# The last stage of a two-layer decoder trunk: output chunks in tiles of their own, an earlier first store, and a root with a bias

## The chip, the cores and the metric

The kernel runs on one NeuronCore of a Trainium2 chip. Its engines work side by side, each through a queue of its own: TensorE (PE, matmuls; PEld are its weight loads), VectorE (DVE), ScalarE (ACT), GpSimd (POOL) and SyncE (SP, which here only issues transfers). [...] The metric is the device time of the whole kernel in microseconds, the median of several runs.

## The reference, cut to what matters

Two layers of token mixers, cross-attention and gated MLPs work on x, 512 tokens of 1024 channels in float32. The change concerns the end of the second layer: the residual add of the last MLP's down projection, and the final norm.

```
h = rms_norm(x, norm) @ w_up
g = causal_dwconv(h[..., :D_FF], dw_w, dw_b)
u = h[..., D_FF:]
x = x + (gelu(g) * u) @ w_down
...
y = x * rsqrt(mean(x * x, axis=-1) + 1e-6)      # per token, over 1024 channels
return y * final_norm                           # per channel
```

## The kernel before, in words

x is kept transposed: eight tiles `X[n]` of 128 channels (partitions) by 512 tokens, all in the one SBUF tile `xall`. Every weight and activation is split into a high and a low part, and each product is three matmuls (`mm3`, lines 185 to 187). Layers, attention and MLP come one after the other; the MLP's gated values are computed in six groups, and the last group's down projection is left to `finish` (line 1098), which is also the final norm. There the 512 tokens are treated in two ways.

*The first 384 tokens* (`TC`) stay transposed. The loop from line 1105 makes, for each of the eight chunks n, 12 matmuls, adds the result to `X[n][:, :TC]` (line 1115, VectorE), squares it (line 1117, ScalarE) and sums the squares over the chunks (line 1122).

*The last 128 tokens* are turned round, tokens on partitions: TensorE transposes their x (line 1113), and `xt`, a 128 by 1024 tile, takes them. The down projection for them comes in four pieces of 256 channels: `last(j)` (line 1128) makes 12 matmuls, and `added(j)` (line 1134) adds the piece to `xt` on VectorE, and squares it on ScalarE with a sum over the piece's channels into column j of the small tile `sm` (in the trace an ACTIVATE and a read of the accumulator). For pieces 0 and 1 GpSimd also multiplies by the channels' gains (line 1139). `count(j)` (line 1141) adds column j-1 to column j, so that column 3 ends as the sum over all channels.

From line 1156 on, the order of the work is written out by hand: within `manual_schedule` each engine, and SP's queue of transfers, executes its instructions in the order of the program text. In that order:

- Piece 0; then 12 small matmuls (line 1161) that sum the squares of the first 384 tokens over the channels, a root (line 1163), a reciprocal (line 1164), and `diagonals` (line 324) and `spread` (line 345), which bring 1/rms of every token to all 128 partitions: two matmuls (line 348) into `r`, a PSUM tile of 128 by 384.
[...]
- `normed(n)` (line 1144) finishes a chunk in its place in x. For n = 3, 5, 7 ScalarE multiplies by the gain (line 1147) and GpSimd by `rs` (line 1148). For the others VectorE does both in one instruction with `r` (line 1150).
- `store(n)` (line 1152) issues one transfer for chunks n and n+1 on SP's queue, 128 partitions by two rows of 1.5 KB. There are four; the first follows chunks 0 and 1.
- Among these stand `added(2)` and `added(3)` and the counts. After count(3) come the root (line 1188, ScalarE), the reciprocal (line 1189, VectorE), and the last multiplications: ScalarE for the first 512 channels (line 1190), VectorE for the rest with the gains (line 1192). One transfer for each half (lines 1191 and 1193) ends the kernel.

VectorE's order there: count(1), normed(0), normed(1), normed(2), added(2), normed(4), count(2), added(3), normed(6), count(3), reciprocal, last multiplication.

Of the kernel before, what the change touches and what calls it, by code (L numbers as in the profile page):

```python
# [12 lines left out]
AF = mybir.ActivationFunctionType  # L13
ALU = mybir.AluOpType

P = 128
T = 512

TC = 384
D = 1024  # L20
C = D // P
# [6 lines left out]
EPS = 1e-6  # L28
# [32 lines left out]
def trunk(ctx: ExitStack, tc: tile.TileContext, I: dict, out: list):  # L61
    nc = tc.nc
    V, A, G, PE = nc.vector, nc.scalar, nc.gpsimd, nc.tensor
# [14 lines left out]
    def nm(s):  # L78
        uid[0] += 1
        return f"{s}_{uid[0]}"  # L80
# [7 lines left out]
    def big_f():  # L88
        return big.tile([P, 2 * T], F32, tag="big", name=nm("big"))
# [4 lines left out]
    def tmp_f(n=T):  # L94
        return tmp.tile([P, n], F32, tag="tmp", name=nm("tmp"))
# [4 lines left out]
    def aux_ps():  # L100
        return aux.tile([P, T], F32, tag="aux", name=nm("aux"))
# [3 lines left out]
    def mm_ps():  # L105

        wide[1] += 1
        return aux_ps() if wide[0] and wide[1] % 7 in (2, 5) else main_ps()

    def stat_ps():  # L110
        return stat.tile([P, T], F32, tag="stat", name=nm("stat"))


    eps = cpool.tile([P, 1], F32, tag="eps", name="eps")
# [4 lines left out]
    xall = xpool.tile([P, C, T], F32, tag="x", name="x")  # L119
    X = [xall[:, c] for c in range(C)]  # L120

    def col(name, i=0):
        j = _COL[name] + i
        return par[:, j : j + 1]
# [21 lines left out]
    def load_w(src=None, eng=None, raw=None, parts=1, ahead=AHEAD, park=False):  # L146

        with tc.high_priority(ahead):
            if raw is None:
                raw = wp.tile([P, D], F32, tag="raw", name=nm("raw"), bufs=3)  # L150
                fetched[0] = nc.sync.dma_start(raw, src)
            if park:
                both = [split(raw[:, i : i + T], None, None, eng) for i in (0, T)]
                return [b[0] for b in both], [b[1] for b in both]
            hi = wp.tile([P, D], F32R, tag="whi", name=nm("whi"))
            lo = wp.tile([P, D], F32R, tag="wlo", name=nm("wlo"))
            n = D // parts
            for i in range(0, D, n):
                split(raw[:, i : i + n], hi[:, i : i + n], lo[:, i : i + n], eng)
        return hi, lo  # L160
# [22 lines left out]
    def mm3(ps, w, x, first, last):  # L183
        (wh, wl), (xh, xl) = w, x
        PE.matmul(ps, wh, xh, start=first, stop=False)  # L185
        PE.matmul(ps, wh, xl, start=False, stop=False)  # L186
        PE.matmul(ps, wl, xh, start=False, stop=last)  # L187
# [16 lines left out]
    def blk(w, i, n=P):  # L204
        hi, lo = (w.hi, w.lo) if isinstance(w, Piece) else w
        if isinstance(hi, list):
            hi, lo, i = hi[i // T], lo[i // T], i % T
        return hi[:, i : i + n], lo[:, i : i + n]
# [27 lines left out]
    class Scaled:  # L236
# [20 lines left out]
        def spread(self):  # L257
            self.r = spread(self.d, unit if self.halves else onesf)
# [65 lines left out]
    def diagonals(rt, n=4, halves=True):  # L324

        def diagonal(out, v, scale):
            V.scalar_tensor_tensor(
                out.rearrange("p (a b) -> p a b", a=n), ident.unsqueeze(1).broadcast_to([P, n, P]), scale,
                v.unsqueeze(2).broadcast_to([P, n, P]), op0=ALU.mult, op1=ALU.mult,
            )  # L330

        if not halves:
            d = [tmp_f(n * P)]
            diagonal(d[0], rt, float(D))
            return d
        hi = small.tile([P, n], F32R, tag="rhi", name=nm("rhi"), bufs=1)
        lo = small.tile([P, n], F32, tag="rlo", name=nm("rlo"), bufs=1)
        d = [act_r()[:, : n * P] for _ in range(2)]
        V.tensor_copy(hi, rt)
        diagonal(d[0], hi.bitcast(F32), 1.0)  # L340
        V.tensor_tensor(lo, rt, hi.bitcast(F32), op=ALU.subtract)
        diagonal(d[1], lo, 1.0)
        return d
# [25 lines left out]
    class Memory:  # L369


        r = rt = None
# [725 lines left out]
    def finish(y, w):  # L1098


        w = [w] + [load_w(I["wdown"][(2 * NG - 1) * (C // 2) + j]) for j in range(1, C // 2)]
        gains = big_f()
        nc.sync.dma_start(gains, I["final_norm"])
        ss, st, xt = None, stat_ps(), big_f()
        for n in range(C):
            x = X[n][:, :TC]
            ps = mm_ps()[:, :TC]
            for k in range(GC):
                mm3(ps, blk(w[n // 2], (k * 2 + n % 2) * P), blk(y[k], 0, TC), k == 0, k == GC - 1)
            if n % 4 == 1:  # L1110
                at, h = aux_ps(), n // 4
                for i in range(4):
                    PE.transpose(at[:, i * P : (i + 1) * P], X[4 * h + i][:, TC:], ident)
                A.activation(xt[:, h * T : (h + 1) * T], at, AF.Copy)
            V.tensor_tensor(x, x, ps, op=ALU.add)
            sq = tmp_f(TC)
            A.activation(sq, x, AF.Square)
            if n == 1:

                A.activation(small.tile([P, 1], F32, tag="warm", name="root", bufs=1), sq[:, :1], AF.Sqrt)  # L1120
            if 0 < n < C - 1:
                V.tensor_tensor(sq, sq, ss, op=ALU.add)
            if n < C - 1:
                ss = sq
        sm = small.tile([P, 5], F32, tag="smt", name="smt", bufs=1)
        H = T // 2

        def last(j):
            ps = mm_ps()[:, :H]
            for k in range(GC):  # L1130
                mm3(ps, blk(y[k], TC), blk(w[j], k * 2 * P, H), k == 0, k == GC - 1)
            return ps

        def added(j, ps):
            at = slice(j * H, (j + 1) * H)
            V.tensor_tensor(xt[:, at], xt[:, at], ps, op=ALU.add)
            A.activation(tmp_f(H), xt[:, at], AF.Square, accum_out=sm[:, j : j + 1])
            if j < 2:
                G.tensor_tensor(xt[:, at], xt[:, at], gains[:, at], op=ALU.mult)

        def count(j):
            V.tensor_tensor(sm[:, j : j + 1], sm[:, j - 1 : j], sm[:, j : j + 1], op=ALU.add)

        def normed(n):
            x, g = X[n][:, :TC], col("final_norm", n)
            if n in (3, 5, 7):
                A.activation(x, x, AF.Copy, scale=g)
                G.tensor_tensor(x, x, rs, op=ALU.mult)
            else:
                V.scalar_tensor_tensor(x, x, g, r, op0=ALU.mult, op1=ALU.mult)  # L1150

        def store(n):
            o = out[0][n : n + 2].rearrange("c p t -> p c t")
            nc.sync.dma_start(o, xall[:, n : n + 2, :TC])

        with tc.manual_schedule(engines=ORDERED | {mybir.EngineType.SP}):
            added(0, last(0))
            n_b = TC // P
            for j in range(n_b):
                for s, first in ((ss, True), (sq, False)):  # L1160
                    PE.matmul(st[:, j : j + 1], s[:, j * P : (j + 1) * P], onesf[:, :1], start=first, stop=not first)
            rt = small.tile([P, 4], F32, tag="rtok", name=nm("rtok"), bufs=2)
            A.activation(rt[:, :n_b], st[:, :n_b], AF.Sqrt, bias=eps)
            V.reciprocal(rt[:, :n_b], rt[:, :n_b])
            d = diagonals(rt[:, :n_b], n_b)
            ps = last(1)
            r = spread(d, ps=aux_ps()[:, :TC])
            added(1, ps)
            rs = tmp_f(TC)
            A.activation(rs, r, AF.Copy)  # L1170
            count(1)
            normed(0)
            normed(3)
            normed(1)
            store(0)
            normed(2)
            normed(5)
            store(2)
            added(2, last(2))
            normed(4)  # L1180
            store(4)
            normed(7)
            count(2)
            added(3, last(3))
            normed(6)
            store(6)
            count(3)
            A.activation(sm[:, 4:], sm[:, 3:4], AF.Sqrt, bias=eps, scale=1.0 / D)
            V.reciprocal(sm[:, 4:], sm[:, 4:])
            A.activation(xt[:, :T], xt[:, :T], AF.Copy, scale=sm[:, 4:])  # L1190
            A.dma_start(out[1][:, :T], xt[:, :T])
            V.scalar_tensor_tensor(xt[:, T:], xt[:, T:], sm[:, 4:], gains[:, T:], op0=ALU.mult, op1=ALU.mult)
            nc.sync.dma_start(out[1][:, T:], xt[:, T:])
# [459 lines left out]
    with tc.manual_schedule(engines=ORDERED | {mybir.EngineType.SP}):  # L1653
# [20 lines left out]
        ps = [[mm_ps(), mm_ps()] for _ in range(2)]  # L1674
# [164 lines left out]
```

## Time and profile before

| | us |
|---|---|
| median of 3 runs (1432.86 to 1433.24) | 1432.87 |
| the profiled execution | 1434.17 |
| its span, first to last instruction | 1432.3 |
| TensorE busy in it (matmuls) | 1419.6 |
| VectorE busy | 1176.7 |
| ScalarE busy | 798.2 |
| GpSimd busy | 304.4 |

The profile is of one execution. Its span counts from the first to the last instruction, and its own time holds what lies around that too, so a sum made in the profile is set against 1434.17 and then carried over to the median. Names as in the text: "x<-x,par,aux" means that an instruction writes tile x and reads x, par and aux; L1150 is line 1150; in timelines the first figure is the start and the second the length in microseconds, and consecutive instructions of one kind may be drawn together (x3).

### The profile page before, as it was taken

Reading aid. Unit: us, or ns where it says so; the run is one execution under the profiler, and the core shown is the slowest. Engines: PE = TensorE matmul, PEld = TensorE weight load, DVE = VectorE, ACT = ScalarE, POOL = GpSimd, SP = SyncE. Lnnn points to the kernel's source line nnn. Section 1 sums busy time; section 2 is a strip of 40 time slices with the busy share of each in tenths; the row PEclk is TensorE's granted clock in tenths of the full one; section 3 lists DMA queues with packets and bytes.
Section 4 is the critical chain, followed back from the end, with each engine's and each line's share of the span. In section 5 each row is a group of like instructions: output and inputs, shape, how many; then the busy total and the mean of one; then the engine's idle time right before and its main releaser. Section 6 shows DMA issues by size and latency. Waiting matters only on the chain.

```text
span 1432.3 us, 22644 instructions
## 1 busy us (share of the span) xinstructions
PE 1419.6 (99%) x8504; PEld 1257.3 (88%) x8504; DVE 1176.7 (82%) x1955; ACT 798.2 (56%) x1321; POOL 304.4 (21%) x317
## 2 busy tenths in 40 slices
PE   9999999999999999999999999999999999999997
PEld 7888888998899999999988777899889999999997
DVE  6987776778788888888888997978778888888885
ACT  7678754666544444544565547767655444444434
POOL 0001310200021221222008992010001222222201
PEclk9999999999999999999999999999999999999999
DMA  8523232542557777777432464345244876787741
GB/s 292 198 81 99 93 118 81 118 111 89 158 136 169 162 182 165 163 173 173 136 123 89 118 167 143 107 87 147 87 129 121 178 179 157 171 184 159 162 126 59
DMA packets 77517, 200.11 MB, mean 140 GB/s; under 512 B 8672, under 2 KB 9952, under 8 KB 77408
## 3 DMA queue, kind: packets, MB, share of 16 engines
q1 hardware_dynamic: 50624, 150.15, 33.6%
q0 software_dynamic: 26496, 48.25, 20.5%
q8 instruction: 67, 1.10, 0.3%
q14 instruction: 42, 0.34, 0.1%
q10 hardware_dynamic: 288, 0.27, 0.1%
HBM read 145.16 MB, written 2.10 MB: 103 GB/s over the span
## 4 chain that ended last, share of the span: by engine, by line
PE 91%; DVE 3%; POOL 2%; DMA 2%; ACT 1%; issue 1%; SPq 0%; POOLq 0%; ACTq 0%; DVEq 0%
PE mm L186 22%; PE mm L185 22%; PE mm L187 22%; PE aux L185 7%; PE aux L186 7%; PE aux L187 7%; PE mm L456 2%; DMA raw<-in_wv 1%; DVE wlo L166 1%; POOL actf L1443 1%; PE aux L529 0%; ACT whi L165 0%; POOL act L166 0%; POOL tmp L1264 0%; DMA raw<-in_win 0%
## 5 line engine op out<-in xcount | busy, mean ns | idle before, releaser
L186 PE MATMUL mm<-act,whi 128*128 128x512 f32 (+2 forms) x1093 | 385.1, 352 | 0.6 <-DVE act L180 0.5
L185 PE MATMUL mm<-act,whi 128*128 128x512 f32 (+2 forms) x1093 | 384.6, 353 | 0.1
L187 PE MATMUL mm<-act,wlo 128*128 128x512 f32 (+2 forms) x1093 | 384.6, 352 | 0.0
L186 PEld LDWEIGHTS mm<-act,whi 128*128 128x128 f32 x1093 | 206.6, 189 | 30.3 <-DVE act L166 1.0
L185 PEld LDWEIGHTS mm<-act,whi 128*128 128x128 f32 x1093 | 206.4, 189 | 30.0 <-ACT tmp L1442 0.8
L187 PEld LDWEIGHTS mm<-act,wlo 128*128 128x128 f32 x1093 | 206.6, 189 | 27.0
L793 ACT ACTIVATE bigr<-raw 128x512 fp32r<-128x512 f32 x160 | 100.7, 630 | 156.7 <-DMA raw<-wa 64.3
L187 PE MATMUL mm<-bigr,bigr 128*128 128x256 f32 x640 | 181.1, 283 | 0.0
L186 PE MATMUL mm<-bigr,bigr 128*128 128x256 f32 x640 | 181.1, 283 | 0.0
L185 PE MATMUL mm<-bigr,bigr 128*128 128x256 f32 x640 | 180.9, 283 | 0.0
L170 DVE TENSOR_TENSOR tmp<-mm,tmp 128x256 f32<-128x256 f32 x322 | 131.2, 420 | 34.7 <-PE mm L187 28.3
L185 PE MATMUL aux<-act,whi 128*128 128x512 f32 x399 | 156.3, 392 | 0.0
L186 PE MATMUL aux<-act,whi 128*128 128x512 f32 x399 | 156.2, 391 | 0.0
L187 PE MATMUL aux<-act,wlo 128*128 128x512 f32 x399 | 155.2, 389 | 0.0
L165 ACT ACTIVATE whi<-raw 128x1024 fp32r<-128x1024 f32 (+1 forms) x95 | 96.6, 1021 | 85.5 <-PE mm L186 44.5
L800 DVE TENSOR_TENSOR bigr<-raw,bigr 128x512 fp32r<-128x512 f32 x160 | 110.0, 688 | 32.4 <-ACT bigr L793 30.4
L186 PEld LDWEIGHTS mm<-bigr,bigr 128*128 128x128 f32 x640 | 122.7, 192 | 1.6
L185 PEld LDWEIGHTS mm<-bigr,bigr 128*128 128x128 f32 x640 | 122.7, 192 | 1.6
L187 PEld LDWEIGHTS mm<-bigr,bigr 128*128 128x128 f32 x640 | 122.7, 192 | 0.0
L803 POOL DMA_DIRECT2D raw<-raw x46 | 39.8, 866 | 350.8 <-DVE wlo L800 303.9
L166 DVE TENSOR_TENSOR wlo<-raw,whi 128x1024 fp32r<-128x1024 f32 (+1 forms) x75 | 90.7, 1212 | 19.7 <-ACT whi L165 19.5
L807 POOL DMA_DIRECT2D raw<-wa x46 | 39.7, 864 | 303.2 <-DVE bigr L800 253.6
(341 smaller groups left out, 3013.4 us busy)
## 6 DMA issues: line engine op xcount, KB each, us to landing
raw<-wa POOLq DMA_DIRECT2D x138, 256.0 KB, 4.4
big<-in_wdown SPq DMA_DIRECT2D x42, 512.0 KB, 6.7
wa<-in_wpair SPq DMA_DIRECT2D x80, 256.0 KB, 3.4
raw<-in_wpair SPq DMA_DIRECT2D x40, 512.0 KB, 5.7
raw<-in_pw SPq DMA_DIRECT2D x24, 512.0 KB, 3.5
raw<-raw POOLq DMA_DIRECT2D x46, 256.0 KB, 7.3
raw<-in_win SPq DMA_DIRECT2D x20, 512.0 KB, 3.4
raw<-in_wk SPq DMA_DIRECT2D x16, 512.0 KB, 3.7
```

Source lines behind the costliest of these rows:

```text
L165: A.activation(hi, src, AF.Copy)
L166: fetched[1] = (eng or V).tensor_tensor(lo, src, hi.bitcast(F32), op=ALU.subtract)
L170: V.tensor_tensor(out, a, b, op=ALU.add)
L185: PE.matmul(ps, wh, xh, start=first, stop=False)
L186: PE.matmul(ps, wh, xl, start=False, stop=False)
L187: PE.matmul(ps, wl, xh, start=False, stop=last)
L456: PE.matmul(p, m[j], x, start=k == 0 and j == 0 and x is hi, stop=k == C - 1 and x is lo)
L793: A.activation(self.w[name][0], self.block(name), AF.Copy)
L800: V.tensor_tensor(lo, self.block(name), hi.bitcast(F32), op=ALU.subtract)
L803: G.dma_start(self.r, self.z, accum_op=ALU.add)
L807: G.dma_start(self.r, self.a22, accum_op=ALU.add)
L1443: G.tensor_tensor(z[:, s:], z[:, s:], f[:, s:], op=ALU.add)
```

## The change

- The finished chunks no longer overwrite x. Four new tiles `done` of 128 by 768 take two chunks each, side by side. The output tensor `out` is laid out the same way, 4 by 128 by 768, so that a store moves one contiguous row of 3 KB on each partition; the host puts the rows back in order.
- The first pair is stored in two halves, chunk 0 as soon as it is there. There are five stores in place of four.
- `rs` is made ahead of piece 1's square, and VectorE's chunks read `rs` in SBUF where they read `r` in PSUM.
- ScalarE's three gain multiplications (`gained`) go ahead of that copy.
- GpSimd's product for piece 1 (`weighed(1)`) goes behind its last chunk.
- VectorE's order becomes: added(1), normed(0), normed(1), normed(2), count(1), normed(4), added(2), normed(6), count(2), a new small instruction, added(3), reciprocal, last multiplication.
- count(3) goes. The new instruction makes (sum of pieces 0 to 2) / 1024 + 1e-6, and the last root takes this as its bias and piece 3's sum, times 1/1024, as its input.

```diff
@@ -1135,26 +1135,32 @@
             at = slice(j * H, (j + 1) * H)
             V.tensor_tensor(xt[:, at], xt[:, at], ps, op=ALU.add)
             A.activation(tmp_f(H), xt[:, at], AF.Square, accum_out=sm[:, j : j + 1])
-            if j < 2:
-                G.tensor_tensor(xt[:, at], xt[:, at], gains[:, at], op=ALU.mult)
 
         def count(j):
             V.tensor_tensor(sm[:, j : j + 1], sm[:, j - 1 : j], sm[:, j : j + 1], op=ALU.add)
 
+        done = [big_f()[:, : 2 * TC] for _ in range(C // 2)]
+
+        def weighed(j):
+            at = slice(j * H, (j + 1) * H)
+            G.tensor_tensor(xt[:, at], xt[:, at], gains[:, at], op=ALU.mult)
+
+        def gained(n):
+            A.activation(X[n][:, :TC], X[n][:, :TC], AF.Copy, scale=col("final_norm", n))
+
         def normed(n):
-            x, g = X[n][:, :TC], col("final_norm", n)
+            x, o = X[n][:, :TC], done[n // 2][:, n % 2 * TC : (n % 2 + 1) * TC]
             if n in (3, 5, 7):
-                A.activation(x, x, AF.Copy, scale=g)
-                G.tensor_tensor(x, x, rs, op=ALU.mult)
+                G.tensor_tensor(o, x, rs, op=ALU.mult)
             else:
-                V.scalar_tensor_tensor(x, x, g, r, op0=ALU.mult, op1=ALU.mult)
-
-        def store(n):
-            o = out[0][n : n + 2].rearrange("c p t -> p c t")
-            nc.sync.dma_start(o, xall[:, n : n + 2, :TC])
+                V.scalar_tensor_tensor(o, x, col("final_norm", n), rs, op0=ALU.mult, op1=ALU.mult)
+
+        def store(n, at=slice(0, 2 * TC)):
+            nc.sync.dma_start(out[0][n // 2][:, at], done[n // 2][:, at])
 
         with tc.manual_schedule(engines=ORDERED | {mybir.EngineType.SP}):
             added(0, last(0))
+            weighed(0)
             n_b = TC // P
...
             d = diagonals(rt[:, :n_b], n_b)
             ps = last(1)
             r = spread(d, ps=aux_ps()[:, :TC])
-            added(1, ps)
+            for n in (3, 5, 7):
+                gained(n)
             rs = tmp_f(TC)
             A.activation(rs, r, AF.Copy)
-            count(1)
+            added(1, ps)
             normed(0)
+            store(0, slice(0, TC))
             normed(3)
             normed(1)
-            store(0)
+            store(0, slice(TC, 2 * TC))
             normed(2)
+            store(2)
+            count(1)
             normed(5)
-            store(2)
-            added(2, last(2))
             normed(4)
             store(4)
+            added(2, last(2))
             normed(7)
-            count(2)
-            added(3, last(3))
             normed(6)
             store(6)
-            count(3)
-            A.activation(sm[:, 4:], sm[:, 3:4], AF.Sqrt, bias=eps, scale=1.0 / D)
+            weighed(1)
+            count(2)
+            V.tensor_scalar(sm[:, 4:], sm[:, 2:3], 1.0 / D, EPS, op0=ALU.mult, op1=ALU.add)
+            added(3, last(3))
+            A.activation(sm[:, 4:], sm[:, 3:4], AF.Sqrt, bias=sm[:, 4:], scale=1.0 / D)
             V.reciprocal(sm[:, 4:], sm[:, 4:])
             A.activation(xt[:, :T], xt[:, :T], AF.Copy, scale=sm[:, 4:])
             A.dma_start(out[1][:, :T], xt[:, :T])
@@ -1829,10 +1839,11 @@
-    shapes = {"out": (C, P, TC), "last": (T - TC, D)}
+    shapes = {"out": (C // 2, P, 2 * TC), "last": (T - TC, D)}
...
-    return np.concatenate([r["out"].reshape(D, TC).T, r["last"].reshape(T - TC, D)], axis=0).reshape(1, T, D)
+    first = r["out"].reshape(C // 2, P, 2, TC).transpose(3, 0, 2, 1).reshape(TC, D)
+    return np.concatenate([first, r["last"].reshape(T - TC, D)], axis=0).reshape(1, T, D)
```

## The prediction

> **What bounds the kernel now.** I read the page's chain of work first, then the chain of the last 14 us in order of time, then the timelines of VectorE, GpSimd, ScalarE and the queues there.
>
> ```profile
> PE 91%; DVE 3%; POOL 2%; DMA 2%; ACT 1%; issue 1%; SPq 0%; POOLq 0%; ACTq 0%; DVEq 0%
> ```
>
> TensorE carries 91% of the chain. The change touches no matmul, so it can only move what stands after the last ones.
>
> ```profile
> 1424.71 0.28 PE L187 MATMUL mm<-whi,act 128*128 128x256 f32 x1
> ```
>
> The last matmul ends at 1424.99 of a span of 1432.3: 7.3 us of tail is the whole stake. A faster tail can't bring more than some of that, and 0.2% of 1432.87, about what a measurement of this kernel can tell from no change, is 2.87 us. The chain through the tail:
>
> ```profile
> 1422.98 1.67 DVE x L1150 x3
> 1424.64 0.34 DVE big L1136
> ...
> 1425.71 0.34 DVE big L1136
> 1426.06 0.02 issue
> 1426.08 0.52 ACT tmp L1137 x2
> 1426.60 0.02 issue
> 1426.62 0.50 DVE smt L1142
> 1427.13 0.02 issue
> 1427.15 0.30 ACT smt L1188
> 1427.45 0.02 issue
> 1427.48 0.17 DVE smt L1189
> ...
> 1427.74 0.72 ACT big L1190
> ```
>
> It is VectorE's queue that sets it: three normed chunks, the addition of piece 2, a normed chunk, a count, the addition of piece 3 (ends at 1426.05); then square, count, root, reciprocal and the weighing, which ends at 1428.46: 2.41 us after that addition. Then come the transfers.
>
> ```profile
> 1424.15 0.41 SPq L1154 DMA_DIRECT2D out<-x  x1
> 1428.49 0.35 ACTq L1191 DMA_DIRECT2D last<-big  x1
> ```
>
> ```profile
> out<-x SPq DMA_DIRECT2D x4, 384.0 KB, 2.9
> ```
>
> ```profile
> 1425.00:1425.25 0.25, 0.00 (x0) 0.00 (x0) 0.25 (x1) 0.24 (x1) 0.25 (x1) 1.00 0.64 227
> 1425.00:1430.75 5.75, 0.00 (x0) 0.00 (x0) 2.92 (x7) 2.55 (x7) 1.51 (x2) 0.83 1.01 363
> ```
>
> The first fence is the queues' timeline, the second a row of the DMA issues (count, size, us to landing), the third a view by windows, whose last two columns are the DMA engines' share and their GB/s. The first store is issued at 1424.15; the window from 1425.00 is 64% full, so bytes flow from about 1425.09, 0.94 us later; and from there to 1430.75 the engines are full at 363 GB/s. The four stores (4 x 384 KB, 1.57 MB) take 4.3 of those microseconds, to about 1429.4. The last transfer, issued at 1428.49, could start 0.94 us later, at 1429.4. So computation and transfers end in a tie: making only one of them earlier gives nothing.
>
> **The change, part by part.** *The factor.* The normed chunks now take `rs` (SBUF) in place of `r` (PSUM), and the copy that makes it goes ahead of piece 1's square.
>
> ```profile
> 1421.68 0.44 PE L348 MATMUL aux<-act,unit 128*128 128x384 f32 x1 [0.16 <-DVE act L327]
> 1422.47 0.47 ACT L1170 ACTIVATE tmp<-aux 128x384 f32<-128x384 f32 x1
> 1422.06 0.42 ACT L1137 ACTIVATE tmp<-big 128x256 f32<-128x256 f32 x1 [2.10 <-DVE big L1136]
> ```
>
> `r` is there at 1422.12, so the copy runs from 1422.16 to 1422.63 and normed(0) starts at 1422.67 instead of 1422.98: 0.31 us gained. The three `gained` copies run in ScalarE's 2.10 us of idle time ahead of L1137 and cost nothing; without that cover they would cost some 0.5 us each.
>
> *VectorE and GpSimd.* The price lies here. Before, a normed chunk on VectorE read x from SBUF and r from PSUM. Now both inputs lie in SBUF, and GpSimd's products read two SBUF inputs at the same time. What the trace shows when both engines do that is in the mixer of the first layer (timeline: start, length, instruction):
>
> ```profile
> 181.25 1.21 DVE L166 TENSOR_TENSOR wlo<-raw,whi 128x1024 fp32r<-128x1024 f32 x1
> 182.38 1.78 DVE L166 TENSOR_TENSOR act<-tmp,act 128x512 fp32r<-128x512 f32 x1
> 181.52 2.08 POOL L1249 TENSOR_TENSOR tmp<-tmp,big 128x512 f32<-128x512 f32 x1 [1.28 <-ACT tmp L1246]
> 183.57 1.74 POOL L1249 TENSOR_TENSOR tmp<-tmp,big 128x512 f32<-128x512 f32 x1
> ```
>
> And two groups of the same sizes from stretches where the two engines were not both reading two SBUF inputs (behind the bar: us in all, then mean ns):
>
> ```profile
> L180 DVE TENSOR_TENSOR act<-tmp,act 128x512 fp32r<-128x512 f32 x6 | 4.2, 693 | 3.2 <-ACT act L175 3.2
> L1443 POOL TENSOR_TENSOR actf<-actf,tmp 128x510 f32<-128x510 f32 x5 | 6.5, 1297 | 0.0
> ```
>
> GpSimd starts at 181.52 while VectorE's L166 runs to 182.46, and ends at 183.60, 1.14 after it; such a product takes 1.30 alone. VectorE's next one, in the queue at 182.38, ends at 184.16, 0.56 after GpSimd; alone it takes 0.69. GpSimd's next ends 1.15 after that. They take turns, each waiting for the whole other one, and the engine that has waited goes next. A turn costs GpSimd its time less 0.15, VectorE its time less 0.13. The end of this kernel shows both sides of the rule:
>
> ```profile
> 1424.04 0.61 DVE L1150 SCALAR_TENSOR_TENSOR x<-x,par,aux 128x384 f32<-128x384 f32 x1
> 1423.53 1.99 POOL L1148 TENSOR_TENSOR x<-x,tmp 128x384 f32<-128x384 f32 x2
> 1425.55 0.16 DVE L1142 TENSOR_TENSOR smt<-smt 128x1 f32<-128x1 f32 x1
> 1426.10 1.00 POOL L1148 TENSOR_TENSOR x<-x,tmp 128x384 f32<-128x384 f32 x1 [0.59 <-ACT x L1147]
> 1426.62 0.49 DVE L1142 TENSOR_TENSOR smt<-smt 128x1 f32<-128x1 f32 x1
> ```
>
> With r in PSUM, L1150 took 0.61 in the midst of GpSimd's product. The count, two SBUF inputs of one element, took 0.49 instead of 0.16 and ended at 1427.11, as GpSimd did.
>
> [...]
>
> The pieces, from the rows of this stage:
>
> ```profile
> L1148 POOL TENSOR_TENSOR x<-x,tmp 128x384 f32<-128x384 f32 x3 | 3.0, 1011 | 0.7 <-ACT x L1147 0.6
> L1139 POOL TENSOR_TENSOR big<-big,big 128x256 f32<-128x256 f32 x2 | 1.5, 737 | 41.3 <-ACT tmp L1137 41.3
> L857 DVE SCALAR_TENSOR_TENSOR tmp<-tmp,par,tmp 128x511 f32<-128x511 f32 x40 | 29.8, 745 | 0.0
> L267 DVE SCALAR_TENSOR_TENSOR actf<-x,par,aux 128x512 f32<-128x512 f32 x16 | 11.9, 746 | 0.6 <-PE aux L348 0.6
> ```
>
> The last two rows say that the place of the second input (SBUF, 745 ns; PSUM, 746) costs nothing by itself, so a normed chunk stays at 0.61, or 0.53 behind another (three in 1.67). A turn is then 0.86 for GpSimd's 384 columns, 0.59 for its 256, 0.48 for a normed chunk, 0.03 for a count. I let VectorE start first, as it began 0.04 us after the copy's end here (if GpSimd does, the same turns end 0.1 later): normed(0) to 1423.28, normed(3) on GpSimd to 1424.14, normed(1) to 1424.62, normed(5) to 1425.48, normed(2) to 1425.96, normed(7) to 1426.82, count(1) to 1426.85, weighed(1) to 1427.44, normed(4) to 1427.92. GpSimd is then done. Three terms more: added(2), which reads PSUM, 0.34, to 1428.26; normed(6), 0.53, to 1428.79; count(2), 0.05 later and 0.16 long, to 1429.00 (its square, begun at 1428.29 and 0.52 long, is done by then). The new small `tensor_scalar` isn't shown; between nothing and twice the reciprocal's 0.17 with its 0.03 of issue, I take that row once: 1429.20. added(3), 0.34, ends at 1429.54 instead of 1426.05: **3.49 us later**. What is queued behind the blocked normed(1), normed(2) and normed(4) on VectorE are the two additions, and for these the last square waits.
>
> *The root with a bias.* Square to root now stay on ScalarE: 0.02 + 0.52 + 0.02 + 0.30, reciprocal 0.02 + 0.17, weighing 0.09 + 0.72: 1.86 in place of 2.41. **0.55 us gained**, of which 0.33 was the count's stall. weighed(1), moved behind normed(7), is done 3 us ahead of its reader.
>
> *Stores.* The first is issued near 1423.3, 0.8 us earlier, and there is one more issue (0.41) on an idle queue. But the last pieces are weighed at 1428.46 + 3.49 - 0.55 = 1431.40, and the stores are out of the way: the last two are issued at 1428.0 (behind normed(4)) and 1428.8 (behind normed(6)), and their bytes are through at about 1430.9, while the last transfer's start is 1432.4. Rows of 3 KB in place of 1.5 KB change only these stores, not the last pieces' own layout: if faster, they gain nothing at the end; if they halved the rate, the last two stores would need 2.2 us each and hold the last transfers up by 0.9 us. I take nothing, by the 363 GB/s that the engines already move. The tail behind the last issue stays at 3.8 us.
>
> **Sum:** +3.49 - 0.55 = +2.94 us. The profiled execution took 1434.17 with a span of 1432.3, so it would become 1437.1; it was 1.30 above the median of 1432.87, which becomes **1435.8**.
>
> **The rivals.**
>
> 1. *Turns in another order.* If normed(4) slips in right behind the one-element count(1), ahead of weighed(1), it ends at 1427.38, added(2) at 1427.72, weighed(1) at 1427.97 and normed(6) at 1428.45: 0.34 less, **1435.5**. [...] Against it: in the rows above the engine that had waited went next.
>
> 2. *Nothing overlaps.* If a blocked instruction takes its full time after the other's end, eight turns lengthen by 0.13 to 0.15 each: some +1.1, **1436.9**. Against it are the 1.14 and 0.56 us above. [...]
>
> [...]
>
> 4. *Not slower: the engines don't block each other here.* [...] It decides as soon as a normed chunk beside GpSimd's product keeps 0.61 us. [...]
>
> **How the numbers follow.** Chances: the turns as worked out 0.50, rival 1 0.20, rival 2 0.08, rival 3 0.08, rival 4 0.07, something upstream that moves with the new tiles and makes it slower still 0.04, a gain that no row shows 0.03. The bound for slower lies at 1435.74. Of the forecast's 0.50, its small terms (0.1 to 0.3 us in the gaps between instructions and the unseen `tensor_scalar`) put about two thirds above it, 0.34; with 0.05 of rival 1, rival 2's 0.08 and the 0.04 that is **0.51 slower**. Within 0.2% lie 0.16 + 0.15 + 0.08 + 0.07 = **0.46**; **0.03** is left for faster. The range runs from rival 3 to rival 2, 1434.0 to 1437.0, and leaves out 0.14.
>
> **What would show it.** Right: GpSimd's three products at 1.3 to 1.4 us each instead of 1.0; normed(1), (2) and (4) on VectorE at 1.3 us or more; added(3) ending some 3.5 us later; DMA engines with gaps before the last stores; no count ahead of the last root. [...] A shift ahead of 1417 us would mean that the new tiles touch earlier work, which I haven't priced.

## The result and the profile after

The changed kernel takes 1435.97 us (median of 16 runs), the kernel before 1432.51 (median of 16 runs between them): a ratio of 1.0022, 95% interval [1.0014, 1.0029], or +3.2 us with an interval from +2.0 to +4.2 (the ratio is taken over all runs; the two medians alone lie 3.5 us apart). The forecast was +2.94 us on 1432.87, a ratio of 1.0021. The change makes the kernel slightly slower.

The profiled execution after has a span of 1433.9 us. The matmuls end at times that differ from execution to execution (1422.2 to 1426.0 among the kernels below), so the tail is read from the end of the last matmul, and "rel." counts from there. The timeline of TensorE after:

```profile
1423.55 0.28 PE L187 MATMUL mm<-whi,act 128*128 128x256 f32 x1
```

The last matmul ends at 1423.83 and the tail is 1433.9 - 1423.83 = 10.1 us, where it was 7.3. That is +2.8 us, and it accounts for the measured difference within its interval; no remainder is shown that the new tiles would have to cause in earlier work.

The chain of work after, in order of time (start, length, what):

```profile
1421.01 0.50 ACT tmp L1177
1421.51 0.02 issue
1421.53 4.03 DVE big L1156 x3
1425.57 0.59 DVE smt L1140
1426.16 0.53 DVE big L1156
1426.69 0.34 DVE big L1136
...
1427.06 0.52 ACT tmp L1137 x2
...
1427.60 0.17 DVE smt L1140
1427.77 0.02 issue
1427.79 0.15 DVE smt L1196
1427.94 0.34 DVE big L1136
1428.28 0.02 issue
1428.31 0.52 ACT tmp L1137 x2
...
1428.85 0.30 ACT smt L1198
...
1429.17 0.17 DVE smt L1199
...
1429.43 0.72 ACT big L1200
```

It is VectorE's queue again, but for piece 2's square on ScalarE, which the second count waits for; that square ends 0.04 us behind VectorE's own last chunk (1427.58 and 1427.54). VectorE's first three normed chunks took 1.67 us before and take 4.03 now. At the end of the list there is no count any more between the last square (L1137) and the last root (L1198). The last addition (L1136) ends at 1428.28 or +4.45 rel., where it ended at +1.06 before.

The timelines of VectorE and GpSimd after, for the same stretch, one instruction to a line and in order of time (start, length, instruction; in brackets the idle time before it and what ended that):

```profile
1421.53 1.48 DVE L1156 SCALAR_TENSOR_TENSOR big<-x,par,tmp 128x384 f32<-128x384 f32 x1 [0.73 <-ACT tmp L1177]
1421.58 1.02 POOL L1154 TENSOR_TENSOR big<-x,tmp 128x384 f32<-128x384 f32 x1 [2.48 <-ACT tmp L1177]
1422.55 1.34 POOL L1154 TENSOR_TENSOR big<-x,tmp 128x384 f32<-128x384 f32 x1
1422.93 1.37 DVE L1156 SCALAR_TENSOR_TENSOR big<-x,par,tmp 128x384 f32<-128x384 f32 x1
1423.85 1.30 POOL L1154 TENSOR_TENSOR big<-x,tmp 128x384 f32<-128x384 f32 x1
1424.22 1.34 DVE L1156 SCALAR_TENSOR_TENSOR big<-x,par,tmp 128x384 f32<-128x384 f32 x1
1425.12 1.03 POOL L1146 TENSOR_TENSOR big<-big,big 128x256 f32<-128x256 f32 x1
1425.49 0.67 DVE L1140 TENSOR_TENSOR smt<-smt 128x1 f32<-128x1 f32 x1
1426.09 0.60 DVE L1156 SCALAR_TENSOR_TENSOR big<-x,par,tmp 128x384 f32<-128x384 f32 x1
```

Both engines start within 0.05 us of each other, behind ScalarE's copy. They then end in turn: GpSimd's products at 1422.60, 1423.89 and 1425.15, VectorE's chunks 0.41 us behind each of them, at 1423.01, 1424.30 and 1425.56. GpSimd's fourth product, on 256 columns, ends at 1426.15. The count on VectorE, of one element, runs beside that fourth product, takes 0.67 us (the later count 0.16) and ends 0.01 behind it. Once GpSimd is through, the next normed chunk takes 0.60, where such a chunk took 0.61 before. The groups of the last 14 us after (behind the bar: us in all, mean ns):

```profile
L1156 DVE SCALAR_TENSOR_TENSOR big<-x,par,tmp 128x384 f32<-128x384 f32 x5 | 5.2, 1080 | 0.7 <-ACT tmp L1177 0.7
L1154 POOL TENSOR_TENSOR big<-x,tmp 128x384 f32<-128x384 f32 x3 | 3.6, 1220 | 2.5 <-ACT tmp L1177 2.5
```

GpSimd's mean was 1011 ns before, and VectorE's 611, as this row of the kernel before says:

```profile
L1150 DVE SCALAR_TENSOR_TENSOR x<-x,par,aux 128x384 f32<-128x384 f32 x5 | 2.9, 611 | 0.2 <-ACT tmp L1170 0.2
```

And the windows after (last two columns: share of the DMA engines, GB/s):

```profile
1424.50:1425.00 0.50, 0.00 (x0) 0.00 (x0) 0.50 (x1) 0.00 (x0) 0.50 (x1) 1.00 0.00 0
1428.00:1429.50 1.50, 0.00 (x0) 0.00 (x0) 0.56 (x3) 0.87 (x4) 0.00 (x0) 0.50 1.02 399
1430.00:1430.50 0.50, 0.00 (x0) 0.00 (x0) 0.12 (x1) 0.15 (x1) 0.00 (x0) 0.50 0.00 0
```

From 1424.5 to 1425.0 nothing moves, for want of finished chunks. The last stores run at 399 GB/s, and from 1430.0 to 1430.5 the DMA engines stand still: every store is out, and the last weighed pieces have only just been issued. The end is set by computation alone now, where before the two ended in a tie.

### The profile page after: what moved, and what is told of

It reads as the page before. It is cut to its first block, busy times and chain, and to the rows that moved or that the text cites. A ratio compares the mean times of both kernels' runs of the same rounds, so it can differ in the third digit from the quotient of the medians.

```text
span 1433.9 us, 22645 instructions
## 1 busy us (share of the span) xinstructions
PE 1418.8 (99%) x8504; PEld 1257.0 (88%) x8504; DVE 1179.5 (82%) x1955; ACT 797.0 (56%) x1321; POOL 305.3 (21%) x317
## 4 chain that ended last, share of the span: by engine, by line
PE 93%; POOL 2%; DVE 2%; ACT 1%; issue 1%; DMA 1%; SPq 0%; POOLq 0%; DVEq 0%; ACTq 0%
PE mm L186 23%; PE mm L185 23%; PE mm L187 23%; PE aux L185 7%; PE aux L186 7%; PE aux L187 7%; PE mm L456 2%; DMA raw<-in_wv 1%; POOL actf L1453 1%; POOL act L166 0%; PE aux L529 0%; DVE wlo L166 0%; POOL tmp L1274 0%; ACT whi L165 0%; DVE big L1156 0%
```

## The experiments

**Theory:** the two engines take turns because the factor that VectorE's chunks read now, `rs`, ScalarE's copy of `r`, lies in SBUF as GpSimd's two inputs do, so VectorE's chunks and additions come late; the other parts of the change move nothing. **Rivals:** the order of VectorE's queue, or the new tiles and stores, cost the time. In the table, "tail" is the profiled span less the end of its last matmul, of one execution each. Half a microsecond is 0.03% of the kernel and less than any interval here can show, so e4 to e6 are read from their tails.

| kernel | tail, us | ratio to before [95%] |
|---|---|---|
| before | 7.3 | |
| after | 10.1 | 1.0022 [1.0014, 1.0029] |
| e1: changed kernel, chunks read the factor in PSUM | 7.5 | 1.0006 [0.9997, 1.0014] |
| e2: kernel before, chunks read the factor in SBUF | 9.3 | 1.0014 [1.0005, 1.0023] |
| e3: changed kernel, all chunks on VectorE | 9.2 | 1.0013 [1.0004, 1.0022] |
| e4: kernel before, last root with a bias | 7.3 | 0.9998 [0.9989, 1.0007] |
| e5: kernel before, contiguous tiles and early store | 7.2 | 1.0000 [0.9991, 1.0009] |
| e6: factor in PSUM, additions first, root with a bias | 6.3 | 0.9998 [0.9989, 1.0007] |
| e7: GpSimd fills instead of multiplying | 7.7 | not timed |
| e8: GpSimd multiplies by the gain, one tensor input | 8.0 | not timed |
| e9: fills, behind the factor | 7.7 | not timed |
| e10: gain products, behind the factor | 7.7 | not timed |

### e1: only the place of the factor taken back

```diff
-                V.scalar_tensor_tensor(o, x, col("final_norm", n), rs, op0=ALU.mult, op1=ALU.mult)
+                V.scalar_tensor_tensor(o, x, col("final_norm", n), r, op0=ALU.mult, op1=ALU.mult)
```

> The changed kernel, but VectorE's normed chunks read the factor from PSUM again; all else as changed. The tail (end of the last matmul to the end of the span) was 7.3 us before and 10.1 after. Theory (the two engines take turns at SBUF): VectorE's five chunks take 0.61 us each, GpSimd's three 1.0 us; only the two counts can still be held up, by 0.3 us at most; tail 7.2 to 7.7 us, total within 0.5 us of the kernel before. Rival (the order: normed(6), two counts and the new small instruction ahead of added(3), or the new tiles and stores): the tail stays at 9.5 us or more and the total some 2.5 us above before.

The groups of e1:

```profile
L1154 POOL TENSOR_TENSOR big<-x,tmp 128x384 f32<-128x384 f32 x3 | 2.9, 1012 | 2.5 <-ACT tmp L1177 2.5
L1156 DVE SCALAR_TENSOR_TENSOR big<-x,par,aux 128x384 f32<-128x384 f32 x5 | 2.9, 607 | 0.7 <-ACT tmp L1177 0.7
```

The chunks read aux (PSUM) and are back at 607 ns, and GpSimd's products at 1012. Order, tiles and stores are those of the changed kernel, and the tail is 7.5 us. So one word of the change carries 2.6 of its 2.8 us, and order, tiles and stores together leave 0.2. The time, +0.9 us with an interval from -0.4 to +2.0, is too wide to check the half microsecond that was expected. The last column shows one thing that was not expected: the first chunk still waited 0.7 us for the copy to `rs`, which it no longer reads. The kernel before has such a wait too (0.2 <-ACT tmp L1170 in its row above, where the chunks read `r`). Why was not tried.

### e2: the same word alone, in the kernel before

```diff
-                V.scalar_tensor_tensor(x, x, g, r, op0=ALU.mult, op1=ALU.mult)
+                V.scalar_tensor_tensor(x, x, g, rs, op0=ALU.mult, op1=ALU.mult)
```

> The kernel before, with one word changed: VectorE's normed chunks read the copy of the factor in SBUF. Theory (turns): normed(2) and normed(4) on VectorE and two of GpSimd's products lengthen to 1.3 us or so, count(2) waits, added(3) comes 2.0 us later and the end 1.65 us later: tail 8.9 us (8.5 to 9.3). Rival (the order or the stores make the loss, the place of the factor costs nothing): tail 7.3 us as before.

The groups of e2, and a line of VectorE's timeline:

```profile
L1150 DVE SCALAR_TENSOR_TENSOR x<-x,par,tmp 128x384 f32<-128x384 f32 x5 | 4.6, 948 | 0.2 <-ACT tmp L1170 0.2
L1148 POOL TENSOR_TENSOR x<-x,tmp 128x384 f32<-128x384 f32 x3 | 3.7, 1257 | 2.0 <-ACT x L1147 1.9
```

```profile
1421.17 3.37 DVE L1150 SCALAR_TENSOR_TENSOR x<-x,par,tmp 128x384 f32<-128x384 f32 x3 [0.22 <-ACT tmp L1170]
```

The same two groups become slow in the old order and the old tiles, 948 and 1257 ns, and the tail grows to 9.3 us: +2.0 from that word alone. It is 0.4 more than the point forecast and at the upper edge of the range on record. The chunks that were held are not those that were expected: normed(0), (1) and (2) together took 3.37 us in place of 1.67, and normed(4) its usual 0.60. In this order the last count, which the root waits for, is held too: it takes 0.82 us where it took 0.49. The two together, 1.70 and 0.33, make the 2.0.

### e3: no GpSimd products

```diff
-            if n in (3, 5, 7):
-                G.tensor_tensor(o, x, rs, op=ALU.mult)
-            else:
+            if True:
                 V.scalar_tensor_tensor(o, x, col("final_norm", n), rs, op0=ALU.mult, op1=ALU.mult)
...
-            for n in (3, 5, 7):
-                gained(n)
```

> The changed kernel, with all eight normed chunks on VectorE (three more than before) and none on GpSimd, the factor still in SBUF. Theory (turns): every chunk takes 0.61 us or 0.53 behind another, save one that meets weighed(1); three more chunks cost 1.6 us and the missing turns give 2.1 back: tail 9.5 us, half a microsecond shorter than the changed kernel in spite of the added work. Rival (a chunk that reads its factor from SBUF is slow on VectorE by itself, 1.3 us): tail 10.1 + 3 x 1.3 = 14 us. Rival (the order alone): 10.1 + 1.6 = 11.7 us.

The groups of e3:

```profile
L1154 DVE SCALAR_TENSOR_TENSOR big<-x,par,tmp 128x384 f32<-128x384 f32 x8 | 5.0, 670 | 0.8 <-ACT tmp L1173 0.8
```

VectorE does eight chunks instead of five, all with two SBUF inputs, and needs 5.0 us for them, less than for the five in the changed kernel (5.2). The tail is 9.2, 0.9 shorter than after. While GpSimd was quiet, chunks with two SBUF inputs kept their usual length (two took 1.14 us): only one chunk, beside `weighed(1)`, took 1.09 us. With the factor in SBUF, GpSimd's help cost more than it brought (a tail of 10.1 with it, 9.2 without); with the factor in PSUM (e1) the tail with its help is 7.5.

### e4: only the root with a bias

```diff
             added(3, last(3))
+            V.tensor_scalar(sm[:, 4:], sm[:, 2:3], 1.0 / D, EPS, op0=ALU.mult, op1=ALU.add)
...
-            count(3)
-            A.activation(sm[:, 4:], sm[:, 3:4], AF.Sqrt, bias=eps, scale=1.0 / D)
+            A.activation(sm[:, 4:], sm[:, 3:4], AF.Sqrt, bias=sm[:, 4:], scale=1.0 / D)
```

> The kernel before, with only the last root changed: it takes the other pieces' sum as its bias, and the small instruction that makes the bias stands behind added(3). The last weighing ends some 0.5 us earlier relative to the last matmul (2.95 us instead of 3.47). Theory of the tie: the DMA engines are full with the four stores until 4.4 us behind the last matmul, so the last transfers can't flow earlier and the tail stays at 7.2 to 7.3 us. Rival: the end follows the last issue by a fixed 3.8 us, tail 6.8 us.

The timeline of e4, and its windows from the end of the last matmul (1422.16 here) on:

```profile
1424.35 0.72 ACT L1190 ACTIVATE big<-big,smt 128x512 f32<-128x512 f32 x1 [0.29 <-DVE smt L1189]
```

```profile
1422.17:1427.67 5.50, 0.00 (x0) 0.00 (x0) 2.47 (x7) 2.53 (x7) 1.50 (x2) 0.84 1.02 365
1427.67:1428.17 0.50, 0.00 (x0) 0.00 (x0) 0.00 (x0) 0.00 (x0) 0.00 (x0) 0.50 0.53 185
```

The weighing ends at 1425.07, +2.91 rel., where it ended at +3.47 before: 0.56 us earlier, as the prediction's part on the root has it (0.55). The tail stays at 7.3. The first window shows why: from the last matmul on the DMA engines are full for 5.5 us without a gap, at 365 GB/s, so the earlier issue only queues behind the stores. The rival, an end 3.8 us behind the last issue, falls: it is 4.4 here. This is one half of the tie.

### e5: only the stores

The kernel before with the four `done` tiles, the new layout of the output and a first store behind normed(0); order, root and the factor in PSUM are left. The edit's main lines:

```diff
             normed(0)
+            store(0, slice(0, TC))
             normed(3)
             normed(1)
-            store(0)
+            store(0, slice(TC, 2 * TC))
```

> The kernel before with the new tiles, the new layout of the output and the first store split in two; VectorE's order, the factor in PSUM and the last root as before. Theory of the tie: the first store is issued 0.5 us earlier, but the last weighing still ends 3.47 us behind the last matmul, so the tail stays at 7.2 to 7.4 us; the DMA engines get a gap before the last transfers. Rival (full DMA engines set the end alone): tail 6.6 to 6.9 us.

The windows of e5 from the end of its last matmul (1426.03):

```profile
1426.03:1428.53 2.50, 0.00 (x0) 0.00 (x0) 2.04 (x6) 1.82 (x6) 1.52 (x2) 1.00 1.04 395
1428.53:1429.03 0.50, 0.00 (x0) 0.00 (x0) 0.47 (x2) 0.26 (x1) 0.00 (x0) 1.00 0.19 68
...
1430.03:1430.53 0.50, 0.00 (x0) 0.00 (x0) 0.00 (x0) 0.00 (x0) 0.00 (x0) 1.00 0.41 152
```

Bytes flow at 395 GB/s, and the engines then have two gaps: one ahead of the last store (a share of 0.19 from 1428.53 on) and one ahead of the last pieces (0.41 from 1430.03 on), whose issue is at +3.50 rel., as before. The tail is 7.2. This is the other half of the tie: faster stores alone gain nothing either.

### e6: what the parts can do together

From the changed kernel: the factor in PSUM, the three additions ahead of the late chunks, and the sum of the pieces put into the root's bias by two small instructions without counts.

```diff
             normed(2)
             store(2)
-            count(1)
+            added(2, last(2))
             normed(5)
             normed(4)
             store(4)
-            added(2, last(2))
             normed(7)
-            normed(6)
-            store(6)
             weighed(1)
-            count(2)
-            V.tensor_scalar(sm[:, 4:], sm[:, 2:3], 1.0 / D, EPS, op0=ALU.mult, op1=ALU.add)
             added(3, last(3))
+            V.tensor_scalar(sm[:, 1:2], sm[:, 1:2], sm[:, 0:1], D * EPS, op0=ALU.add, op1=ALU.add)
+            V.tensor_scalar(sm[:, 4:], sm[:, 2:3], sm[:, 1:2], 1.0 / D, op0=ALU.add, op1=ALU.mult)
+            normed(6)
+            store(6)
```

> A version meant to beat both: the changed kernel with the factor read from PSUM on VectorE, the additions of pieces 2 and 3 ahead of normed(4) and normed(6), and the two counts and the small instruction merged into two that read one SBUF tile and a per-partition scalar. Expected: no VectorE instruction is held up by GpSimd; the last weighing ends 2.5 us behind the last matmul (3.47 before, 6.3 changed) and, since the stores have started earlier too, the tail is 6.3 us, 1.0 less than before. Rival (full DMA engines hold the last transfers): tail 6.8 us or more. Total 0.5 to 1.5 us below before.

The timeline of e6 (its last matmul ends at 1424.79):

```profile
1425.26 0.21 DVE L1190 TENSOR_SCALAR smt<-smt 128x1 f32<-128x1 f32 x1
1425.57 0.21 DVE L1191 TENSOR_SCALAR smt<-smt 128x1 f32<-128x1 f32 x1
...
1426.50 0.72 ACT L1196 ACTIVATE big<-big,smt 128x512 f32<-128x512 f32 x1 [0.29 <-DVE smt L1195]
```

The last weighing ends at 1427.22, +2.43 rel., and the tail is 6.3 us, 1.0 below before and 3.8 below after. Now both sides of the tie move, and the end moves with them. 1.0 us is 0.07% of the kernel, and the ratio of 0.9998 [0.9989, 1.0007] can't tell it from no change. The 0.5 to 1.5 us in the total that were expected are therefore not shown. e6 is faster than the changed kernel (whose interval begins at 1.0014), and its gain over the kernel before is shown in the tail's profile only.

### e7 and e8: what on GpSimd does the blocking

In the changed kernel, GpSimd's product (the factor `rs` at 384 columns) is replaced: in e7 by two fills, which read nothing, in e8 by a product with the gain, which reads one tensor. In e7 to e10 three chunks of the output are thus not computed, and only the profiles are read.

```diff
-                G.tensor_tensor(o, x, rs, op=ALU.mult)
+                G.memset(o, 0.0)
+                G.memset(o, 0.0)
```

```diff
-                G.tensor_tensor(o, x, rs, op=ALU.mult)
+                G.tensor_scalar(o, x, col("final_norm", n), None, op0=ALU.mult)
```

> The changed kernel, factor in SBUF, but GpSimd fills its three chunks with zeros twice each instead of multiplying x by the factor; these three chunks aren't computed. [...] Rival (any GpSimd instruction on SBUF blocks VectorE): chunks lengthen by GpSimd's 0.4 us each, tail 8.6 us or more.

> The changed kernel, factor in SBUF, but GpSimd multiplies its three chunks by the per-partition gain only (one SBUF input of 384 columns, a per-partition scalar, no factor); these three chunks aren't normed. [...] Rival (only two-input products on GpSimd block): chunks stay at 0.61 us, tail 7.4 to 8.2 us.

The timeline of e7:

```profile
1419.91 0.42 POOL L1155 MEMSET big<- 128x384 f32 x1
...
1420.52 2.15 DVE L1157 SCALAR_TENSOR_TENSOR big<-x,par,tmp 128x384 f32<-128x384 f32 x3 [0.73 <-ACT tmp L1178]
```

Both are inconclusive, by a fault of their making. The replacements don't read the factor, so GpSimd didn't wait for it: e7's last fill ended at 1420.33, before VectorE's first chunk began, and of the 4.04 us of e8's three products only the last 1.7 lay beside the chunks. The tails, 7.7 and 8.0, say that without turns the changed order costs little. 8.0 lies in the range of e8's rival, that only two-input products block, and e7's 7.7 below the 8.6 where its rival begins; but with so little beside the chunks neither says which GpSimd instruction blocks.

### e9 and e10: the same, held back until the factor is there

A first product of one column reads `rs`, so that the rest waits for it.

```diff
-                G.tensor_tensor(o, x, rs, op=ALU.mult)
+                G.tensor_tensor(o[:, :1], x[:, :1], rs[:, :1], op=ALU.mult)
+                G.memset(o[:, 1:], 0.0)
+                G.memset(o[:, 1:], 0.0)
```

In e10 one `G.tensor_scalar(o[:, 1:], x[:, 1:], col("final_norm", n), None, op0=ALU.mult)` stands in place of the two fills.

> As the run in which GpSimd only writes zeros, but each pair of fills now stands behind a product of one column with the factor, so that the fills can't run ahead of VectorE's chunks; GpSimd's three chunks aren't computed. [...] Rival (any GpSimd instruction on SBUF blocks): three of VectorE's chunks take 1.3 us or more, tail 9.3 us or more.

> As the run in which GpSimd multiplies its three chunks by the gain only (one SBUF input), but each behind a product of one column with the factor, so that they run beside VectorE's chunks; these three chunks aren't normed. In the run without that, one chunk took 0.94 us beside a GpSimd product of 1.32 us and one 0.62 beside the last 0.4 us of another. [...] Rival (one input doesn't block): chunks of 0.61 us, tail 7.6 to 8.3 us.

The groups of e9:

```profile
L1158 DVE SCALAR_TENSOR_TENSOR big<-x,par,tmp 128x384 f32<-128x384 f32 x5 | 2.9, 613 | 0.7 <-ACT tmp L1179 0.7
```

With fills beside them nearly all the time (and three one-column products of 0.2 to 0.3 us between these), VectorE's chunks take 613 ns, although both their inputs lie in SBUF. So the fills, which only write, did not hold VectorE up here (its chunks took 611 ns in the kernel before).

The timelines of e10:

```profile
1421.15 2.03 DVE L1157 SCALAR_TENSOR_TENSOR big<-x,par,tmp 128x384 f32<-128x384 f32 x3 [0.73 <-ACT tmp L1178]
1421.37 1.56 POOL L1155 TENSOR_SCALAR big<-x,par 128x383 f32<-128x383 f32 x1
1421.72 0.93 DVE L1157 SCALAR_TENSOR_TENSOR big<-x,par,tmp 128x384 f32<-128x384 f32 x1
...
1423.17 0.62 DVE L1157 SCALAR_TENSOR_TENSOR big<-x,par,tmp 128x384 f32<-128x384 f32 x1
1423.20 1.62 POOL L1155 TENSOR_SCALAR big<-x,par 128x383 f32<-128x383 f32 x1
...
1424.04 0.61 DVE L1157 SCALAR_TENSOR_TENSOR big<-x,par,tmp 128x384 f32<-128x384 f32 x1
...
1424.96 1.25 POOL L1155 TENSOR_SCALAR big<-x,par 128x383 f32<-128x383 f32 x1
```

The 0.93 is the second of the three chunks drawn together in the first line. The author's estimates for e10 were chunks longer by 0.3 to 0.9 us and a tail of 8.3 to 9.8, or, if a product held a chunk for its whole length, chunks of 1.7 and a tail of 10.5 or more; both missed. The product with one tensor input takes 1.56 us, but the three chunks beside it take 2.03 together, only 0.36 more than three undisturbed ones (1.67), and nearly all of that fell on one chunk of 0.93. The next two chunks, 0.62 and 0.61, ran to their usual length beside another such product. GpSimd pays too: its two products beside two-input chunks took 1.56 and 1.62, the third, beside none, 1.25. The tail is 7.7, in the range of the rival that one input doesn't block; but the chunk of 0.93 does not fit that rival, and part of the tail is GpSimd's own lateness, as the last weighing waits for `weighed(1)` (0.7 us idle <-POOL). So the price depended on GpSimd's instruction: its two-input products held each of three chunks to 1.34 us or more (after; 0.61 by itself), its product with the gain one chunk to 0.93. Whether the one tensor less makes the difference, or the other kind of instruction (1.25 us by itself in place of 1.01), was not tried.

## Why the prediction was right, point by point

- **The stake and the tie held.** The tail moved by 2.8 us, and the whole time by as much within its interval. e4 makes the computation 0.56 us earlier, e5 the stores faster; neither moves the end alone, e6 moves both and gains 1.0 us.
- **The factor earlier: right.** normed(0) starts at 1421.53, -2.30 rel., against a forecast of -2.32 (1422.67 - 1424.99) and -2.01 before. The three gain multiplications are hidden: they take ScalarE 1.62 us, and 0.69 of idle time follows before its copy to `rs`.
- **The turns: right in kind and sum, not in detail.** GpSimd took the first turn, which the prediction had put in brackets at 0.1 us more: its first product ran at 1.02 us and VectorE's first chunk was held to 1.48. GpSimd's other two took 1.34 and 1.30, as forecast (0.88 and 0.85 behind VectorE's chunk, forecast 0.86). VectorE's turn was mis-sized, 0.41 where the prediction took 0.48. `weighed(1)` went right behind normed(2) and not behind the count, so the three held chunks were normed(0), (1) and (2), and normed(4) ran free at 0.60 where at least 1.3 was forecast. The sum was hardly touched, as the two errors point opposite ways, which is in part luck: normed(4) ends at 1426.69, +2.86 rel., forecast +2.93.
- **added(3): 3.39 us later, forecast 3.49.** The small `tensor_scalar` takes 0.15, the forecast took 0.17.
- **The root: 0.54 gained, forecast 0.55.** From the end of added(3), 1428.28, to the end of the weighing, 1430.15, are 1.87 us instead of 2.41.
- **Stores and transfers: nothing, as forecast, but not by the forecast's course.** The first store was to be issued 0.8 us earlier. It is issued at 1423.04, -0.79 rel., and was at -0.84 before: its chunk is the one that GpSimd held. Nothing hung on it, as the end is set by computation. The gaps before the last stores are there (1424.5 to 1425.0). The rows of 3 KB do move faster (399 GB/s against 363), which the forecast left open, and gain nothing at the end. The last issue to the span's end is 3.7 us, 0.1 less than taken.
- **The sum:** 3.39 - 0.54 - 0.1 = +2.75 in the profile, forecast +2.94; the timed ratio puts it between +2.0 and +4.2, which can't tell these apart. Nor can it say on which side of the prediction's bound of 0.2% the change lies (1.0014 to 1.0029): with 0.51 against 0.46 the prediction called that nearly even, and 1.0022 does not settle it.
- **The rivals.** Rival 1 (normed(4) ahead of `weighed(1)`) fell by the order above. Rival 2 (no overlap at all) fell by the tail, for which it wanted some 1.1 us more, and by the turns: a held chunk ended 0.41 us behind GpSimd's product, less than its own 0.61. Rival 3, which gives the range its lower end of 1434.0, was the author's estimate for VectorE's first five instructions in a row ahead of all GpSimd's products; no run shows that order, and the order of the ends speaks against it: GpSimd took the first turn, and after each of the first two held chunks one of its products came before VectorE's next. Rival 4 (no blocking) fell by 1080 ns in place of 611, and e1 shows the kernel as it would be then: with the blocking gone the tail is 7.5, 0.2 over before, where the author's estimate was 0.1.

## What to carry to other kernels

Before an operand of a VectorE instruction with two tensor inputs is moved from PSUM to SBUF, look at which instructions GpSimd runs at that moment: beside GpSimd's two-input products each of the three held chunks cost some 0.8 us more (4.03 for three in place of 1.67) and three of GpSimd's four products 0.3, while VectorE's instruction by itself shows no difference (613 ns in e9, 611 before). When computation and transfers end in a tie, price a change by the later of the two; a real gain on one side (0.56 us here) shows as nothing. And when work is shared between two engines that take turns, check whether the shared stretch is shorter than the one engine alone: with the factor in SBUF it was not (a tail of 10.1 after, 9.2 in e3). Leaving the factor in PSUM (e1) removed the turns between chunks and products altogether (607 ns a chunk, 1012 a product).

## What the runs showed of the hardware

- Between VectorE's two-input chunks and GpSimd's two-input products the turns alternated: a held chunk ended 0.41 us behind GpSimd's product (0.61 by itself), a held product 0.85 to 0.88 behind VectorE's chunk (1.01 by itself; after).
- GpSimd's fills beside VectorE's two-input chunks cost these nothing (613 ns in e9), and its one-input products held one chunk to 0.93 us, a third of a microsecond more than usual (e10), and were themselves lengthened from 1.25 to 1.56 and 1.62, where its two-input products held three chunks to 4.03 us (after).
- e1's chunks take their gain as one scalar for each partition, with x in SBUF and the factor in PSUM, and ran at 607 ns beside GpSimd's products: no hold shows. The second of e6's small `TENSOR_SCALAR`, which takes such a scalar from SBUF, needed 0.21 us and ended 0.4 us ahead of the GpSimd product beside it (0.15 us for the one in the changed kernel, which takes constants); the first ended together with a GpSimd product, and so shows nothing. The counts of one element with two tensor inputs beside GpSimd's products needed 0.67 (after) and 0.82 (e2), where one alone took 0.16.
- Stores of one 3 KB row on each partition, in the new layout, ran at 395 to 399 GB/s (e5, after), those of two 1.5 KB rows at 363 to 364 (before from 1425.50 to 1429.25, e4 from 1422.67 to 1426.17). Whether the row or the layout in memory makes the difference was not tried.
- GpSimd took the first turn although the profile has its product begin 0.05 us after VectorE's chunk (1421.58 and 1421.53): there the recorded starts do not say who came first.
